# A two-layer streaming encoder step: after the attention, work that VectorE or GpSimd could do goes to VectorE alone; the norms add their squares with two additions

## The chip, the cores and the metric

The kernel runs on one core of one Trainium2 chip. The engines are named as the profile names them: PE is TensorE (matmuls; PEld is its weight load), DVE is VectorE, ACT is ScalarE, POOL is GpSimd, SP is SyncE, which issues the DMAs. The metric is device time in microseconds (us) of one execution, lower is better.

## The reference, cut to what matters

One inference step of two layers, for a prompt of 2048 frames and a sample of 32 frames with caches. D_MODEL is 1024, all data is f32.

```python
for l in range(DEPTH):                      # 2 layers
    hp = rms_norm(yp, ln_pre[l]); hs = rms_norm(ys, ln_pre[l])
    if l % 2 == 0:                          # layer 0: attention
        qa, ka, va, ga, qb, kb, vb, gb = ab_project(hp, pos_p, w_in_ab[j])
        oa = prompt_band(qa, ka, va, N_PREV_A, None, sinks_a[j])        # 8 heads, 2 KV heads, rotary, sinks
        ob = prompt_band(qb, kb, vb, N_PREV_B, relpos_b[j], None)       # 8 heads, learned bias
        mp = ab_output(oa, ob, ga, gb, w_out_ab[j])  # concat(oa*silu(ga), ob*silu(gb)) @ w_out
        ...                                 # the same for the sample, with caches
    else:                                   # layer 1: recurrence
        mp, h_last, conv_last = lru_mixer(hp, ...)
        ...
    yp = yp + rms_norm(mp, ln_post[l]); ys = ys + rms_norm(ms, ln_post[l])

def rms_norm(x, g):
    y = xf * lax.rsqrt(jnp.mean(xf * xf, axis=-1, keepdims=True) + EPS)
    return y * g

def lru_mixer(h, conv_state, h0, w_in, ...):
    xb, z = jnp.split(h @ w_in, 2, axis=-1)
    xc = conv_b + sum of 4 taps of xb * conv_w          # width-4 causal depthwise convolution
    r, gi = sigmoid(block-diagonal xc @ wa + ba), sigmoid(block-diagonal xc @ wx + bx)
    log_a = C_GATE * r * log_sigmoid(lam); a = exp(log_a)
    u = sqrt(-expm1(2 * log_a)) * (gi * xc)
    hs = scan of  h = a * h + u                         # along time
    return (hs * silu(z)) @ w_out, ...
```

## The kernel before, in words

Prompt and sample stand side by side as 2084 columns (tokens), with the 1024 channels on the partitions in 8 tiles of 128. The columns are cut into 6 blocks of 352 (the last 324), and two blocks make one part, b = 0, 1, 2. Each dense product is done with operands split in a high and a low piece: a weight tile of 128 output channels is `wh` and `wl` (`wh` is the weight rounded to the matmul's type, `wl` what is left), an input is `r0h`/`r0l` or `r1h`/`r1l`, and a result of one block is 8 channel tiles x 3 products (high x high, high x low, low x high) = 24 matmuls of 128x352 into an accumulator `acc` in PSUM.

The order of all instructions is made when the program is built, by a list scheduler (class `Sched`). Every piece of the work is a generator that yields requests (`R`) for an engine; the scheduler keeps an own clock per engine with a table of costs (`cost`), asks the waiting generators by priority, and gives a request to an engine when its inputs and buffers are ready. Where a request names two engines, `("V", "G")` for DVE or POOL or `("A", "V")` for ACT or DVE, `pick` takes the one that would end first by that table. Nothing is decided on the chip; each engine works through its own list in order, and waits on semaphores. All instructions go through one helper line, so the profile puts them all on L101, and groups are told apart by the names of the tiles.

The stages, by the program:

- Layer 0's input product for three parts, and the attention beside it and behind it (`soft`, `transp`: scores `S`, softmax rows `pt`, transposes `T`, outputs `O`). The key ("attention",) is set when the last attention piece has been scheduled. In the profile the last `pt` row is at 994 us.
- Layer 0's output product, parts 0 to 2 (`out_part`). `fin_out` takes each accumulator: ACT scales it into `m` and squares it (`tz`, `tzb`), the squares are added into `sacc`, and at the end of a block PE sums `sacc` over the partitions (`norm_sum`, by way of the split `xs`, into PSUM `misc`), ACT takes the root into `r`, DVE inverts it, and `m` is multiplied by `r` and the residual (`xr`, `eti`, `xt`) is added, in pieces of 5 and 3 channel tiles (880 and 528 columns). The weights of these stages still have to be split: `w_split` makes `wh` on ACT or DVE and `wl` on DVE or POOL, 1024 columns each, from the staged tile `wst`. There are three `wh`/`wl` pairs.
- `y_proc` makes the inputs of that product for parts 1 and 2 (products `xt<-xt`, `ex<-ex`, then the split into `r1h`/`r1l` or `r0h`/`r0l`).
- Layer 1, three times `in_part` and `out_part`. `in_part` is the input product with, for each of 8 channel tiles c: `fin_x` (ACT copies the accumulator to `xb`, DVE makes the convolution from `xb` in four instructions into a tile `xc`, which is shown as `ex`; split into `xs`; gate matmuls `g` with `gh`/`gl`; gates on ACT; the scan on DVE; the split into `r0h`/`r0l`), and `fin_z2` (the SiLU gate, which frees the accumulator on DVE). There is one `xb` buffer. The weights of part 0 are split here too, and stored for parts 1 and 2.
- `norm_proc` is the norm ahead of a layer, for one part: ACT squares half of a tile of [128, 8, 176] into `sq` (one buffer, 4 channel tiles x 176 columns), DVE sums it over the 4 channel tiles into `ss`, four times per block, then `norm_sum`, root, reciprocal and 8 scalings per piece. It runs for parts 1 and 2 in layer 0 and for parts 0 to 2 ahead of layer 1.

PE's list has no other source than this scheduler: when a weight or an accumulator is late, PE stands.

Of the kernel before, what the change touches and what calls it, by code (L numbers as in the profile page):

```python
# [12 lines left out]
OP = mybir.AluOpType  # L13
AX = mybir.AxisListType
# [45 lines left out]
def _cols(ap):  # L60
    n = 1
    for x in ap.shape[1:]:
        n *= x
    return n
# [19 lines left out]
class Eng:  # L84


    def __init__(self, sch, name, eng):
        self.sch, self.name, self.eng = sch, name, eng
# [77 lines left out]
class Sched:  # L166
# [3 lines left out]
    def __init__(self):  # L170
        self.t = {"PE": 0.0, "A": 0.0, "V": 0.0, "G": 0.0, "SP": 0.0, "DMA": 0.0}
        self.w, self.r, self.key = {}, {}, {}
        self.procs = []
        self.now = 0.0
        self.n = 0
        self.tab = None
        self.lock = {"V": [], "G": []}
        self.win, self.busy, self.half = 0, 0.0, False
        self.pem, self.vpt = PEMA, VPTA
        self.halves, self.cuts, self.loaded = set(), {}, set()  # L180
# [16 lines left out]
    def cost(self, e, op, outs, ins, a, k):  # L197
        n = max(_cols(x) for x in outs + ins) if e != "PE" else 0
        if e == "PE":
            m = ins[1]  # L200
            w = _cols(m)
            if op == "transpose":
                return ins[0].shape[0] / 1200.0 + 0.004
            return max(w / 2400.0 + 0.0133, 0.108) if m.dtype == F32R else 4 * w / 2400.0
        if e == "A":
            c = (0.104 if all(str(x.space).endswith("SB") for x in ins[:1]) else 0.067) + n / 1200.0 + 0.093 * sum(hasattr(k.get(x), "tensor") for x in ("scale", "bias", "accum_out"))
            f = a[2] if op == "activation" else None
            tab = "sqrt" if f == AF.Sqrt else "exp" if f in (AF.Exp, AF.Tanh) else None
            if tab and tab != self.tab:
                c += 1.3  # L210
                self.tab = tab
            return c
        if e == "V":
            if op == "reciprocal":
                return 0.06 + n * 0.0066
            if op in ("tensor_copy", "tensor_scalar", "memset") and all(str(x.space).endswith("SB") for x in outs + ins):
                return 0.06 + n * 0.00053 + self.vpt * sum(_cols(x) == 1 for x in ins[1:])
            if op == "tensor_tensor_scan":
                return 0.1 + n * 0.00115
            return 0.06 + n * 0.00106 + self.vpt * sum(_cols(x) == 1 for x in ins[1:])  # L220
        if op in ("tensor_scalar", "memset"):
            return 0.1 + n * 0.00106
        return 0.1 + n * 0.00223
# [57 lines left out]
    def set(self, key, t=None):  # L281
        self.key[key] = self.now if t is None else t
# [38 lines left out]
    def pick(self, req):  # L321

        t = self.avail(req)
        if t is None:
            return None
        if req.eng[0] == "SP" and req.ins and not isinstance(req.ins[0], tuple):
            t += SPM
        best = None
        for i, e in enumerate(req.eng):
            if e == "PE":  # L330
                if t <= self.now + EPSR / 2:
                    best = (0, e)
                continue
            if self.t[e] > self.now + LOOK[e] or t > max(self.now, self.t[e]) + EPSR:
                continue
            f = max(self.t[e], t) + (req.cost[i] if req.cost else 0.0) + (VPEN if e == "V" else 0.0)
            if best is None or f < best[0]:
                best = (f, e)
        if best and req.func and self.tab and req.func != self.tab:

            if req.since is None:
                req.since = self.now
            if self.now < req.since + 1.0:
                return None
        return best and best[1]
# [49 lines left out]
def hybrid_kernel(ctx, tc, I, O):  # L395
    nc = tc.nc
    sch = Sched()
    V, A, G, PE, SP = [Eng(sch, n, e) for n, e in (("V", nc.vector), ("A", nc.scalar), ("G", nc.gpsimd),
                                                  ("PE", nc.tensor), ("SP", nc.sync))]
# [215 lines left out]
    def cells_of(b):  # L615
        return [(bi, T0[2 * b + bi] + off, bi * BLK + off, w) for bi in range(2) for off, w in subs(2 * b + bi)]
# [43 lines left out]
    def norm_proc(src, b, gi, ri, key, rings, free=None, after=None, src_ready=(), then=None, blocks=(0, 1)):  # L660

        if after is not None:
            yield R("SP", [lambda: after])
        cells = cells_of(b)

        def block(bi, xs):
            cc = cells[2 * bi:2 * bi + 2]
            sa, sb = yield R("A", [xs[0]], [ssr, ssr])
            offs = [0, cc[0][3]]
            tot = cc[0][3] + cc[1][3]  # L670
            for x, (_, _, _, w), o in zip(xs, cc, offs):
                for ss, ks in ((sa, slice(0, 4)), (sb, slice(4, 8))):
                    sq, = yield R("A", [x], [sqr])
                    A.activation(sq[:, :, :w], x[:, ks, :w], AF.Square)
                    yield R("V", [sq])
                    V.tensor_reduce(ss[:, o:o + w], sq[:, :, :w].rearrange("p k t -> p t k"), AX.X, OP.add)
                    sqr.release(sq)
            e, _ = yield R(("G", "V"), [sa, sb], cost=(0.89, 0.43))
            ENG[e].tensor_tensor(sa[:, :tot], sa[:, :tot], sb[:, :tot], OP.add)
            ssr.release(sb)  # L680
            ps = yield from norm_sum(sa[:, :tot])
            r = sa
            yield R("A", [ps], func="sqrt")
            A.activation(r[:, :tot], ps[:, :tot], AF.Sqrt, bias=epsT, scale=1.0 / D)
            psr_.release(ps)
            for x, (_, _, _, w), o in zip(xs, cc, offs):
                yield R("V", [r])
                V.reciprocal(r[:, o:o + w], r[:, o:o + w])
                for k0 in (0, 4):
                    yield R("V", [r])  # L690
                    for k in range(k0, k0 + 4):
                        V.scalar_tensor_tensor(x[:, k, :w], x[:, k, :w], vec[:, gi, k:k + 1], r[:, o:o + w], OP.mult, OP.mult)
            ssr.release(sa)

        idx = [2 * bi + j for bi in blocks for j in range(2)]
        xs = {}

        def load(i, g):
            xs[i], = yield R("SP", src_ready, [g])
            x_load(xs[i], src, cells[i][1], cells[i][3])  # L700
        early = len(rings) == len(idx)
        for i, g in zip(idx, rings):
            yield from load(i, g)
        if early:
            for bi in blocks:
                yield from block(bi, [xs[2 * bi], xs[2 * bi + 1]])
        for bi in blocks:
            ii = (2 * bi, 2 * bi + 1)
            if not early:
                if bi == 1:  # L710
                    for i, g in zip(ii, rings):
                        yield from load(i, g)
                yield from block(bi, [xs[i] for i in ii])
            t = 0.0
            for i in ii:
                t = max(t, (yield from split_R(xs[i], cells[i][3], ri, cells[i][2], [(free, bi)] if free else [])))
                rings[idx.index(i) % len(rings)].release(xs[i])
            sch.set((key, bi), t)
        if then:
            then()  # L720
# [1229 lines left out]
    def dense_2():  # L1950
        for b in range(3):
            yield from out_part(b, base + 8 * b, b % 2, I["xT"], LN_POST, x2T, lambda k, bi, b=b: (("y", b), bi), late_m=b > 0)
            if b == 0:

                yield R("PE", [("attention",)])
        spawn(gw_proc(), 1)
        xrr.retire(eti)
        for x in extra:
            xtr.retire(x)
        b1 = base + 24  # L1960
        for b in range(3):
            yield from in_part(b, b1 + 24 * b, 1, 0)
            if b < 2:
                spawn(norm_proc(x2T, b + 1, LN_PRE + 1, 1, (1, b + 1), [xtr, xtr], free=("in", b), src_ready=[("x2", b + 1)]), PY3)
            yield from out_part(b, b1 + 24 * b + 16, 0, x2T, LN_POST + 1, O["yT"], lambda k, bi, b=b: ("yc", b, k), late=True, final=b == 2)
# [29 lines left out]
    ar, szr = [Ring(sch, None, None, None, t, 1, tiles=[x]) for t, x in zip(("a", "sz"), parts[1])]  # L1995
    xtr.idle += [(0.0, -1, x) for x in extra]
    sch.set(("attention",))
    sch.pem, sch.vpt = PEM, VPT
    spawn(y_proc(1, 1, ("y", 1), then=y2), PY2)
    sch.run(lambda: not sch.procs)  # L2000
# [114 lines left out]
```

## Time and profile before

| what | us |
|---|---|
| median of 3 runs | 1881.93 (1880.21 to 1882.59) |
| the profiled execution | 1876.91 |
| its span, first to last instruction | 1875.1 |
| what lies around the span | 1.8 |
| busy in the span: PE, DVE, ACT, POOL | 1743.0, 1590.4, 1002.5, 610.6 |

The profiled execution is 5.0 us below the median of the runs. PE is busy 93% of the span, but matmuls overlap, so this is no measure of how full PE is: where PE runs without a break a 352-column matmul starts every 0.16 us and each is shown with 0.32 us. PE's idle time and the granted clock (`PEclk`, a share of full speed) are what can be read.

A row of a table by stages gives for each stretch its length, the busy time of each engine (x instructions), the granted clock and the DMA share. A row of a table by tile gives engine, operation, what is written from what, how often, and the least, the median and the largest duration in ns. A row of waits gives who waited for whom, the sum in us, how often and the longest.

### The profile page before, as it was taken

Reading aid. Unit: us, or ns where it says so; the run is one execution under the profiler, and the core shown is the slowest. Engines: PE = TensorE matmul, PEld = TensorE weight load, DVE = VectorE, ACT = ScalarE, POOL = GpSimd, SP = SyncE. Lnnn points to the kernel's source line nnn. Section 1 sums busy time; section 2 is a strip of 40 time slices with the busy share of each in tenths; the row PEclk is TensorE's granted clock in tenths of the full one; section 3 lists DMA queues with packets and bytes.
Section 4 is the critical chain, followed back from the end, with each engine's and each line's share of the span. In section 5 each row is a group of like instructions: output and inputs, shape, how many; then the busy total and the mean of one; then the engine's idle time right before and its main releaser. Section 6 shows DMA issues by size and latency. Waiting matters only on the chain. (4 is left out here: it accounts for less than half of the span.)

```text
span 1875.1 us, 31799 instructions
## 1 busy us (share of the span) xinstructions
PE 1743.0 (93%) x11078; PEld 1686.8 (90%) x11078; DVE 1590.4 (85%) x3168; ACT 1002.5 (53%) x2048; POOL 610.6 (33%) x433
## 2 busy tenths in 40 slices
PE   8999999999999999999989969989889999999995
PEld 7999999889899999999979959988889999998995
DVE  8999967999999679989897879799898988699943
ACT  4276632476657337656564343456663586447831
POOL 4332214322223232221242646654423320153112
PEclk8999999999999999999999979999889999999997
DMA  5798856887554487877765884585455834565376
GB/s 177 205 252 262 233 151 211 228 249 211 168 157 119 128 237 186 245 202 203 212 190 153 225 231 134 191 258 175 154 174 186 238 121 149 182 200 167 128 269 177
DMA packets 293577, 362.80 MB, mean 193 GB/s; under 512 B 36309, under 2 KB 244617, under 8 KB 293401
## 3 DMA queue, kind: packets, MB, share of 16 engines
q1 hardware_dynamic: 293416, 360.78, 65.3%
q8 instruction: 87, 1.43, 0.3%
q14 instruction: 74, 0.60, 0.1%
HBM read 255.77 MB, written 107.00 MB: 193 GB/s over the span
## 5 line engine op out<-in xcount | busy, mean ns | idle before, releaser
L101 PE MATMUL acc<-r0h,wh 128*128 128x352 f32 (+2 forms) x1832 | 594.6, 325 | 16.3 <-ACT r0h L101 6.6
L101 PE MATMUL acc<-r0l,wh 128*128 128x352 f32 (+2 forms) x1832 | 595.1, 325 | 1.3 <-DVE r0l L101 1.3
L101 PE MATMUL acc<-r0h,wl 128*128 128x352 f32 (+2 forms) x1832 | 594.4, 324 | 1.5 <-DMA wl<-wo1s 1.5
L101 PEld LDWEIGHTS acc<-r0h,wh 128*128 128x128 f32 x1832 | 348.3, 190 | 19.4 <-ACT r0h L101 7.2
L101 PEld LDWEIGHTS acc<-r0l,wh 128*128 128x128 f32 x1832 | 348.2, 190 | 3.2 <-DVE r0l L101 2.2
L101 PEld LDWEIGHTS acc<-r0h,wl 128*128 128x128 f32 x1832 | 348.2, 190 | 3.2 <-DMA wl<-wo1s 2.5
L101 PE MATMUL acc<-r1h,wh 128*128 128x352 f32 (+1 forms) x864 | 282.8, 327 | 22.4 <-ACT xb L101 14.1
L101 PE MATMUL acc<-r1h,wl 128*128 128x352 f32 (+1 forms) x864 | 281.1, 325 | 15.2 <-POOL wl L101 15.2
L101 PE MATMUL acc<-r1l,wh 128*128 128x352 f32 (+1 forms) x864 | 281.0, 325 | 0.0
L101 POOL TENSOR_SCALAR pt<-pt,rr 128x256 f32<-128x256 f32 (+4 forms) x142 | 100.0, 715 | 366.2 <-DVE rr L101 214.3
L101 POOL TENSOR_TENSOR wl<-wst,wh 128x1024 fp32r<-128x1024 f32 x62 | 155.6, 2509 | 186.3 <-ACT wh L101 109.3
L101 ACT ACTIVATE pt<-pt,nm 128x256 f32<-128x256 f32 (+6 forms) x272 | 169.7, 626 | 61.2 <-DVE nm L101 59.3
L101 PEld LDWEIGHTS acc<-r1h,wh 128*128 128x128 f32 x864 | 166.1, 192 | 25.4 <-ACT xb L101 16.1
L101 PEld LDWEIGHTS acc<-r1h,wl 128*128 128x128 f32 x864 | 165.8, 192 | 15.5 <-POOL wl L101 15.5
L101 ACT CAST pp<-T 128x256 fp32r<-128x256 f32 (+4 forms) x314 | 134.0, 438 | 84.7 <-PE T L101 66.0
L101 PEld LDWEIGHTS acc<-r1l,wh 128*128 128x128 f32 x864 | 166.2, 192 | 0.0
L101 PE MATMUL T<-ident,pt 128*128 128x128 f32 (+2 forms) x864 | 143.4, 274 | 18.3 <-DVE pp L101 10.3
L101 DVE TENSOR_TENSOR pp<-T,pp 128x256 fp32r<-128x256 f32 (+4 forms) x314 | 150.4, 496 | 7.8 <-ACT pp L101 6.0
L101 PE MATMUL O<-pp,vt 128*128 128x256 f32 (+3 forms) x728 | 135.8, 309 | 10.0 <-DVE pp L101 4.7
L101 PEld LDWEIGHTS T<-ident,pt 128*128 128x128 f32 (+2 forms) x864 | 101.7, 140 | 42.7 <-DVE pp L101 19.9
L101 ACT CAST wh<-wst 128x1024 fp32r<-128x1024 f32 x70 | 73.5, 1049 | 99.7 <-PE acc L101 72.9
L101 PE MATMUL S<-kk,qa 128*128 128x320 f32 (+5 forms) x376 | 120.3, 334 | 3.6 <-issue 1.6
(252 smaller groups left out, 3312.8 us busy)
## 6 DMA issues: line engine op xcount, KB each, us to landing
wst<-w_in SPq DMA_DIRECT2D x93, 512.0 KB, 4.3
wst<-wo_in SPq DMA_DIRECT2D x32, 512.0 KB, 4.4
wh<-w1s SPq DMA_DIRECT2D x32, 512.0 KB, 3.7
wl<-w1s SPq DMA_DIRECT2D x32, 512.0 KB, 4.6
wh<-wo1s SPq DMA_DIRECT2D x24, 512.0 KB, 3.8
wl<-wo1s SPq DMA_DIRECT2D x24, 512.0 KB, 4.6
kk<-kB SPq DMA_DIRECT2D x32, 320.0 KB, 4.9
vt<-vB SPq DMA_DIRECT2D x16, 640.0 KB, 4.8
```

The costliest lines, as they stand in the source:

```text
L101: r = fn(*a, **k)
```

## The change

Three edits. First, the scheduler has a switch `alone`. While it is on, a request that names several engines is not given to POOL (requests that name POOL alone still are). It is set when the attention's end is reached, and in layer 1 it is turned off while an `in_part` has been issued and the following `out_part` is being issued: so it is on for layer 0's remaining output products, the norms between, and the three `in_part`s, and off for the three `out_part`s of layer 1. Second, in `norm_proc` the sum over 4 channel tiles, one strided `tensor_reduce` over 704 elements, becomes two additions: tiles 0 and 1 plus tiles 2 and 3 (352 columns, in place), then the two halves (176 columns). Third, the scheduler's table gets an own cost for the `tensor_reduce` that is left, in the first norm. The first edit as it acts in the order: 149 two-engine instructions leave POOL's list behind the attention, 23 stay.

```diff
@@ class Sched
+        self.alone = False
...
+            if op == "tensor_reduce":
+                return 0.06 + n * 0.00195
...
@@ pick
+            if e == "G" and len(req.eng) > 1 and self.alone:
                 continue
...
@@ norm_proc
                     yield R("V", [sq])
-                    V.tensor_reduce(ss[:, o:o + w], sq[:, :, :w].rearrange("p k t -> p t k"), AX.X, OP.add)
+                    V.tensor_tensor(sq[:, 0:2, :w], sq[:, 0:2, :w], sq[:, 2:4, :w], OP.add)
+                    V.tensor_tensor(ss[:, o:o + w], sq[:, 0, :w], sq[:, 1, :w], OP.add)
...
@@ dense_2
         for b in range(3):
+            sch.alone = True
             yield from in_part(b, b1 + 24 * b, 1, 0)
+            sch.alone = False
...
     sch.set(("attention",))
+    sch.alone = True
```

Since the scheduler's table decides the whole order, the rows move everywhere; buffer numbers differ from the start. Three places matter here.

**Layer 0's output product, part 1, the end of part 0's blocks.** POOL's list before (`m` is the product's output, `r` its inverse root, `eti` and `xr` the residual, `r0l` a low piece of part 2's input, `wl` the low piece of a weight):

```order
L101 TENSOR_TENSOR m_1_10371<-m_1_10371,r_0_10374 128x5x176
L101 TENSOR_TENSOR r0l_150<-ex1_0_10792,r0h_149 128x4x176
L101 TENSOR_TENSOR m_1_10371<-m_1_10371,r_0_10374 128x5x176
L101 TENSOR_TENSOR m_1_10371<-m_1_10371,eti_0_10782 128x5x176
L101 TENSOR_TENSOR r0l_150<-xt_0_151,r0h_149 128x4x176
L101 TENSOR_TENSOR sacc_0_10372<-sacc_0_10372,tzb_0_10779 128x352
L101 TENSOR_TENSOR m_1_10371<-m_1_10371,xr_0_153 128x5x176
L101 TENSOR_TENSOR r0l_150<-xt_1_152,r0h_149 128x4x176
L101 TENSOR_TENSOR wl_2_124<-wst_1_118,wh_2_121 128x1024
```

The same `wl` in DVE's list of the change:

```order
L101 RECIPROCAL r_0_10390<-r_0_10390 128x176
L101 TENSOR_TENSOR m_0_10386<-m_0_10386,xr_0_153 128x5x176
L101 TENSOR_TENSOR m_1_10387<-m_1_10387,r_0_10390 128x5x176
L101 TENSOR_TENSOR m_1_10387<-m_1_10387,r_0_10390 128x3x176
L101 RECIPROCAL r_0_10390<-r_0_10390 128x176
L101 TENSOR_TENSOR m_0_10386<-m_0_10386,xr_0_153 128x3x176
L101 TENSOR_TENSOR m_1_10387<-m_1_10387,r_0_10390 128x5x176
L101 TENSOR_TENSOR m_1_10387<-m_1_10387,r_0_10390 128x3x176
L101 TENSOR_TENSOR xt_0_151<-xt_0_151 128x704
L101 TENSOR_TENSOR wl_2_124<-wst_1_118,wh_2_121 128x1024
```

The `wl` was the last of a row of POOL's work that DVE shared; now it stands in one list with all of it, behind all eight products with `r` and four additions, ahead of the four other additions.

**The norm ahead of layer 1, part 0.** DVE's list before:

```order
L101 TENSOR_REDUCE ss_0_155<-sq_0_154 128x176
L101 TENSOR_REDUCE ss_1_156<-sq_0_154 128x176
L101 TENSOR_TENSOR sacc_0_10372<-sacc_0_10372,tzb_0_10779 128x352
L101 TENSOR_REDUCE ss_0_155<-sq_0_154 128x176
L101 TENSOR_REDUCE ss_1_156<-sq_0_154 128x176
```

and in the change:

```order
L101 TENSOR_TENSOR sq_0_154<-sq_0_154 128x352
L101 TENSOR_TENSOR ss_0_155<-sq_0_154 128x176
L101 TENSOR_TENSOR sq_0_154<-sq_0_154 128x352
L101 TENSOR_TENSOR ss_1_156<-sq_0_154 128x176
L101 TENSOR_TENSOR sacc_0_10388<-sacc_0_10388,tzb_0_10795 128x352
L101 TENSOR_TENSOR sq_0_154<-sq_0_154 128x352
L101 TENSOR_TENSOR ss_0_155<-sq_0_154 128x176
L101 TENSOR_TENSOR sq_0_154<-sq_0_154 128x352
L101 TENSOR_TENSOR ss_1_156<-sq_0_154 128x176
L101 TENSOR_TENSOR ss_0_155<-ss_0_155,ss_1_156 128x352
```

Each reduction is two rows, and the addition of the two halves `ss`, which stood on POOL, follows on DVE.

**Layer 1's first `in_part`.** POOL's list before held the weights' and the gates' low pieces and half of the splits `xs`:

```order
L101 TENSOR_TENSOR wl_0_122<-wst_1_118,wh_0_119 128x1024
L101 TENSOR_TENSOR xs_1_10789<-ex0_0_10791,xs_1_10789 64x704
L101 TENSOR_TENSOR wl_1_123<-wst_0_117,wh_1_120 128x1024
L101 TENSOR_TENSOR gl_0_10786<-gst_0_10790,gh_0_10785 128x256
L101 TENSOR_TENSOR wl_2_124<-wst_1_118,wh_2_121 128x1024
L101 TENSOR_TENSOR xs_0_10788<-ex0_0_10791,xs_0_10788 64x704
```

In the change they stand in DVE's list, between the convolution's instructions (`ex0<-xb,vec`):

```order
L101 TENSOR_TENSOR gl_0_10802<-gst_0_10806,gh_0_10801 128x256
L101 COPY hist_135<-xb_0_10803 128x3
L101 TENSOR_SCALAR ex0_0_10807<-xb_0_10803,vec_125 128x704
L101 TENSOR_TENSOR wl_0_122<-wst_1_118,wh_0_119 128x1024
L101 SCALAR_TENSOR_TENSOR ex0_0_10807<-xb_0_10803,vec_125,ex0_0_10807 128x704
L101 TENSOR_TENSOR wl_1_123<-wst_0_117,wh_1_120 128x1024
L101 SCALAR_TENSOR_TENSOR ex0_0_10807<-xb_0_10803,vec_125,ex0_0_10807 128x704 x2
L101 CAST xs_0_10804<-ex0_0_10807 64x704
L101 CAST xs_1_10805<-ex0_0_10807 64x704
L101 TENSOR_TENSOR xs_0_10804<-ex0_0_10807,xs_0_10804 64x704
```

Two `wl` have moved in among the four instructions that hold the one `xb`.

More of the change, by code (lines that the diff above doesn't have):

```diff
@@ L332, in pick @@
                     best = (0, e)
+                continue
+            if e == "G" and len(req.eng) > 1 and self.alone:
                 continue
```

## The prediction

> **What bounds the kernel now.** I read the page's first part, then the table by stages, then PE's waits in the stretch that the change reaches, then the tile tables and the timeline of the engines that PE waits for.
>
> ```profile
> span 1875.1 us, 31799 instructions
> PE 1743.0 (93%) x11078; PEld 1686.8 (90%) x11078; DVE 1590.4 (85%) x3168; ACT 1002.5 (53%) x2048; POOL 610.6 (33%) x433
> ```
>
> By the page PE bounds, DVE is close behind, and POOL is idle two thirds of the time, which would make it the engine to give work to. The stages tell more. Columns: stretch, length, busy PE, PEld, DVE, ACT, POOL, clock, DMA.
>
> ```profile
> 0.00:1000.00 1000.00, 956.18 (x6275) 912.88 (x6276) 876.11 (x2337) 550.06 (x1356) 286.70 (x261) 0.99 0.70 199
> 1000.00:1100.00 100.00, 84.52 (x524) 83.90 (x523) 79.33 (x64) 35.61 (x68) 57.85 (x28) 0.93 0.80 226
> 1100.00:1230.00 130.00, 119.86 (x733) 118.29 (x732) 109.70 (x113) 50.07 (x88) 76.83 (x41) 0.96 0.62 183
> 1230.00:1367.00 137.00, 119.95 (x701) 117.83 (x700) 125.70 (x130) 92.55 (x118) 63.35 (x30) 0.94 0.57 193
> 1367.00:1440.00 73.00, 63.51 (x362) 61.79 (x361) 60.66 (x82) 34.76 (x56) 13.41 (x9) 0.91 0.52 179
> 1440.00:1575.00 135.00, 128.17 (x785) 126.38 (x784) 121.31 (x150) 84.87 (x112) 39.16 (x23) 0.99 0.53 162
> 1640.00:1775.00 135.00, 129.54 (x824) 127.54 (x824) 126.96 (x185) 89.79 (x144) 46.48 (x27) 1.00 0.55 168
> 1775.00:1876.00 101.00, 77.10 (x491) 74.86 (x489) 44.32 (x52) 30.04 (x57) 20.32 (x10) 0.89 0.68 212
> 1000.00:1876.00 876.00, 786.78 (x4805) 773.94 (x4803) 714.28 (x832) 452.43 (x694) 323.92 (x172) 0.95 0.60 187
> ```
>
> The first row is the part up to the attention's end. 1000 to 1230 is the rest of layer 0's output product, 1230 to 1367, 1440 to 1575 and 1640 to 1775 are the three in_parts, 1367 to 1440 an out_part, and the last 101 us the last out_part. Behind the attention PE is idle for 876.0 - 786.8 = 89 us, and up to 1440 the clock is lowered as well. DVE and POOL together are busy 714.3 + 323.9 = 1038 us in 876. Whom PE waits for there, with the sum, the count and the longest:
>
> ```profile
> PE acc L101 <- POOL wl L101: 15.2, 1, 15.2
> PE acc L101 <- ACT xb L101: 14.1, 6, 4.9
> PE acc L101 <- DVE ex L101: 8.3, 3, 4.7
> PE acc L101 <- ACT r0h L101: 6.6, 2, 5.7
> PE g L101 <- DVE xs L101: 6.4, 7, 1.6
> PE misc L101 <- DVE xs L101: 6.1, 2, 5.8
> ...
> PE misc L101 <- POOL xs L101: 1.1, 1, 1.1
> ```
>
> These make 57.8 us; nearly all end with DVE or POOL, since xb is copied by ACT only when DVE has finished with the one buffer. So PE stands for the pair DVE and POOL. Now the pair, by tile, with the least, median and largest duration in ns:
>
> ```profile
> L101 POOL TENSOR_TENSOR wl<-wst,wh x24: 2372/2548/3253, 1020.9 to 1402.4; 128x1024 fp32r<-128x1024 f32 x24
> L101 DVE TENSOR_TENSOR wl<-wst,wh x20: 1209/1224/3149, 1006.2 to 1417.3; 128x1024 fp32r<-128x1024 f32 x20
> L101 DVE TENSOR_TENSOR m<-m,r x24: 1004/2332/2671, 1059.0 to 1861.8; 128x880 f32<-128x880 f32 x10, 128x528 f32<-128x528 f32 x10, 128x810 f32<-128x810 f32 x3, 128x486 f32<-128x486 f32 x1
> L101 POOL TENSOR_TENSOR m<-m,r x24: 1326/2217/2835, 1058.8 to 1863.6; 128x528 f32<-128x528 f32 x10, 128x880 f32<-128x880 f32 x10, 128x486 f32<-128x486 f32 x3, 128x810 f32<-128x810 f32 x1
> L101 DVE TENSOR_TENSOR m<-m,xr x15: 696/1078/2195, 1065.7 to 1697.4; 128x880 f32<-128x880 f32 x9, 128x528 f32<-128x528 f32 x4, 128x810 f32<-128x810 f32 x2
> L101 POOL TENSOR_TENSOR xs<-ex,xs x19: 1640/2233/2478, 1246.2 to 1771.9; 64x704 fp32r<-64x704 f32 x12, 64x676 fp32r<-64x676 f32 x7
> L101 DVE TENSOR_TENSOR xs<-ex,xs x29: 855/886/2020, 1235.1 to 1772.8; 64x704 fp32r<-64x704 f32 x20, 64x676 fp32r<-64x676 f32 x9
> L101 POOL TENSOR_TENSOR gl<-gst,gh x22: 737/1316/1874, 1220.9 to 1770.1; 128x256 fp32r<-128x256 f32 x22
> L101 DVE TENSOR_TENSOR gl<-gst,gh x2: 425/426/426, 1548.0 to 1749.0; 128x256 fp32r<-128x256 f32 x2
> L101 DVE SCALAR_TENSOR_TENSOR ex<-xb,vec,ex x72: 844/946/3075, 1230.9 to 1769.9; 128x704 f32<-128x704 f32 x48, 128x676 f32<-128x676 f32 x24
> L101 DVE TENSOR_TENSOR sacc<-sacc,tz x29: 459/518/2725, 1000.8 to 1842.3; 128x352 f32<-128x352 f32 x23, 128x324 f32<-128x324 f32 x6
> ```
>
> POOL takes about twice DVE's time for the same work, and DVE's own instructions have two durations: m with r is 1.0 us at the least and 2.3 in the median. The timeline shows which (start and length in us):
>
> ```profile
> 1062.42 2.79 POOL L101 TENSOR_TENSOR m<-m,r 128x880 f32<-128x880 f32 x1 [2.17 <-DVE r L101]
> 1063.19 2.58 DVE L101 TENSOR_TENSOR m<-m,r 128x528 f32<-128x528 f32 x1
> 1320.47 3.06 POOL L101 TENSOR_TENSOR wl<-wst,wh 128x1024 fp32r<-128x1024 f32 x1 [0.73 <-ACT wh L101]
> 1321.22 3.08 DVE L101 SCALAR_TENSOR_TENSOR ex<-xb,vec,ex 128x704 f32<-128x704 f32 x1
> ```
>
> A DVE instruction that meets one of POOL's lasts until POOL's is over and then its own time: 1062.42 + 2.79 = 1065.21, and 0.6 us more is DVE's end at 1065.77; likewise 1323.53 and 0.8 more. So with two SBUF inputs the two take turns, and what POOL does is paid by DVE at POOL's slower rate. DVE's 714 us hold much of such waiting.
>
> **The change part by part.** *DVE alone.* 149 instructions leave POOL (the part on the change counts them): 23 wl, 40 additions and products on m, 19 xs, 22 gl, 25 others of 648 to 704 columns, 16 sacc, 4 smaller. On DVE, undisturbed: 23 x 1.22 + 40 x 0.85 (half way between 1.0 for 880 columns and 0.7 for 528) + 44 x 0.886 + 22 x 0.426 + 20 x 0.52 = 28.1 + 34.0 + 39.0 + 9.4 + 10.4 = 121 us, in place of some 285 of POOL's 323.9 (23 stay, at 1.7 us or so, between the medians of gl and of m). That is 0.42 us for each us of POOL. It is free only if DVE's waiting falls by as much. I can't sum that waiting from one row. Bounds: at the most all 285, at the least none; from the m and r row alone (24 x about 1.5 us over the 0.7 to 1.0 undisturbed) come 28, and the rows of xb and wl show the same tail, so I take about 100, and expect DVE as busy as now.
>
> What PE gains, wait by wait:
>
> - The wl wait. PE stood from 1075 to 1090:
>
> ```profile
> 1087.71 2.81 POOL L101 TENSOR_TENSOR wl<-wst,wh 128x1024 fp32r<-128x1024 f32 x1
> 1090.57 0.66 PE L101 MATMUL acc<-r1h,wl 128*128 128x352 f32 x1 [15.21 <-POOL wl L101]
> 1057.43 1.25 DVE L101 RECIPROCAL r<-r 128x176 f32<-128x176 f32 x1 [2.28 <-ACT r L101]
> ```
>
>   In the new list this wl stands 18 instructions behind the first reciprocal: 4 reciprocals x 1.25, 6 m of 880 columns x 1.0, 6 of 528 x 0.7, 2 of 704 x 0.886, the wl 1.22, together 18.2 us. From 1057.4 that is 1075.6, when PE runs dry. The wait falls from 15.2 to between 0 and 4: 13. Late next is the following wl, three rows on (3.0 us); a weight feeds 48 matmuls (7.7 us), so it is in time.
> - xb and ex, 14.1 + 8.3 = 22.4. All have the convolution or the gate product stretched ahead of them (the 3.08 above instead of 0.95, ahead of a PE wait of 4.9). Bounds: 0, since two wl now stand among the four convolution instructions (2 x 1.22), and 19. Half: 11.
> - misc on xs, 6.1 + 1.1. The second edit and the addition of ss on DVE shorten the chain ahead of it: 3.
> - r0h, g on xs (6.6 + 6.4): chains with one or two POOL pieces in them; a third: 4.
> - The clock. (1 - clock) x length is 7.0 + 5.2 + 8.2 + 6.6 = 27 us up to 1440, part of it inside the waits. It is low around them. With about half the waits gone: 4.
>
> Sum 13 + 11 + 3 + 4 + 4 = 35.
>
> Against that, DVE's one list. Priced without any relief, moved POOL time x 0.42 on DVE's busy time against the stretch: 1230 to 1367, 125.7 + 26.6 = 152 for 137, +15; 1100 to 1230, 109.7 + 32.3 = 142 for 130, +12; 1640 to 1775, 127.0 + 19.5 = 146.5 for 135, +11.5; 1000 to 1100, +3.6; 1440 to 1575, 137.8 for 135, +2.8. That is 45 at the worst. The relief covers it on average; since work now queues in front of each other I charge a fifth: 9. Layer 1's out_parts keep POOL, and the last 101 us are as before.
>
> *The two additions.*
>
> ```profile
> L101 DVE TENSOR_REDUCE ss<-sq x40: 1268/1429/1469, 137.8 to 1633.9; 128x176 f32<-128x704 f32 x32, 128x162 f32<-128x648 f32 x8
> L101 DVE SCALAR_TENSOR_TENSOR xt<-xt,vec,ss x112: 373/391/2554, 162.5 to 1646.6; 128x176 f32<-128x176 f32 x96, 128x162 f32<-128x162 f32 x16
> ```
>
> The 352-column addition is priced by sacc, 0.52; the 176-column one by the nearest row, 0.39: 0.91 for 1.43, so 0.5 less, 40 times, 20 us of DVE, of which a wait shows only the misc item. 16 of the 40 lie ahead of 1000, where PE is busy 96%: worth 1, between 0 and 8.
>
> [...]
>
> *The cost of tensor_reduce* and all else that the new order reshuffles ahead of 1000: 0, within 5 either way; POOL's list there is 10 shorter. The sum is 35 + 1 - 9 = 27 against the profiled 1876.9, so 1850; the median of the runs stands 5.0 above that execution: 1855.
>
> **The rivals.**
>
> *DVE becomes the bound (slower).* If DVE's stretching is not POOL's doing, or what is saved goes to worse queueing, the 45 above are paid and the wl wait is still saved: 1881.9 + 45 - 13 = 1914; with half the relief 1892. It decides in the in_parts: above 135 us of DVE in 135 it wins. For it speaks that DVE is already at 127 there; against it the two-fold durations above. [...] Chance 0.14.
>
> *Hidden anyway.* The waits only move: PE runs dry elsewhere, xb is held longer by the wl among the convolution. Then the wl wait (13) and the charge (9) remain: 4 gained, 1878. For it: in_part's PE share is already 95% from 1440 on. Chance 0.16, of which 0.06 within 0.2%.
>
> *All of it.* The charge is nothing, the xb and ex waits go but 3, the clock is back: 15 + 19 + 5 + 8 + 8 = 55 gained, 1827. Chance 0.08.
>
> **How the numbers follow.** The forecast, 12 to 45 us gained, 1837 to 1870, has 0.62. 0.2% is 3.8 us, about what a measurement of this kernel tells from no change. Faster by more: 0.62 + 0.08 + 0.10 of the second rival = 0.80; within: 0.06; slower: 0.14. The range for 8 in 10: 1834, where the full gain begins to count, to 1881, which takes in the hidden case.
>
> **What would show it.** In the changed kernel's profile: POOL busy about 40 us behind the attention; m with r at 0.7 to 1.1 on DVE in layer 0; DVE busy 680 to 750 there; no PE wait on wl over 5 us; the convolution's largest under 2 us in the in_parts; reductions replaced by pairs of about 0.9. Wrong it would be if DVE is above 95% in an in_part with PE's waits on xb longer than 22 us in sum, or if the part ahead of 1000 moved by more than 8 us.

## The result, and the profile after

The changed kernel took 1833.27 us in the median of 4 runs (1827.26 to 1840.37), the kernel before 1882.26 us beside it: a ratio of 0.9743, 95% interval 0.9705 to 0.9781. On another chip, later, it was 0.9767 (0.9740 to 0.9794). The forecast was 1855.0, from 1834 to 1881: the direction was right, and the gain, 49 us, was nearly twice the 27 forecast and 0.7 us beyond the range. The profiled execution took 1835.62 us, 2.3 above that median; the one of before stood 5.4 below its own, so the two profiles differ by 41 us and not by 49. Two single executions further down, one of 4075 us and one of 2128, stand far off the others of their kernels and are not counted.

The page's first part:

```profile
span 1833.8 us, 31731 instructions
PE 1735.4 (95%) x11078; PEld 1678.0 (92%) x11078; DVE 1547.9 (84%) x3372; ACT 1001.9 (55%) x2045; POOL 316.6 (17%) x274
```

The table by stages with the columns of before (stretch, length, busy PE, PEld, DVE, ACT, POOL, clock, DMA), cut at the same events, and last everything behind the attention's end in one row:

```profile
0.00:1009.50 1009.50, 957.67 (x6275) 913.39 (x6276) 882.37 (x2358) 553.27 (x1361) 277.42 (x251) 0.99 0.70 197
1009.50:1106.00 96.50, 92.87 (x574) 91.97 (x573) 75.54 (x99) 40.22 (x74) 0.94 (x1) 0.98 0.88 251
1106.00:1217.00 111.00, 107.98 (x685) 107.40 (x684) 97.25 (x158) 48.21 (x85) 0.00 (x0) 1.00 0.64 192
1217.00:1330.00 113.00, 105.42 (x642) 101.90 (x641) 108.03 (x156) 88.82 (x112) 0.00 (x0) 1.00 0.63 217
1330.00:1400.00 70.00, 68.48 (x417) 67.95 (x416) 58.15 (x96) 34.86 (x57) 10.68 (x7) 0.98 0.67 228
1400.00:1536.00 136.00, 129.90 (x786) 126.45 (x785) 120.28 (x176) 84.45 (x110) 2.72 (x2) 0.99 0.52 160
1600.00:1733.00 133.00, 131.09 (x828) 129.08 (x827) 122.79 (x212) 88.71 (x145) 2.63 (x2) 1.00 0.56 171
1733.00:1834.00 101.00, 78.01 (x483) 75.89 (x481) 41.52 (x50) 29.03 (x54) 16.72 (x8) 0.90 0.66 212
...
1009.50:1834.00 824.50, 777.75 (x4805) 764.65 (x4803) 665.56 (x1015) 448.66 (x686) 39.14 (x23) 0.98 0.63 199
```

Two things stand here. Behind the attention the same 4805 matmuls take 824.5 us instead of 876.0, and DVE, which took over 149 instructions, is busy 665.6 us instead of 714.3: less, not more. The clock, 0.91 to 0.96 up to the first out_part before, is 0.98 to 1.00. And the first row, 6275 matmuls as before, now needs 1009.5 us instead of 1000: the part that the switch doesn't reach lost 9.5 us. PE's waits behind the attention (sum, count, longest):

```profile
PE g L101 <- DVE xs L101: 9.6, 13, 3.3
PE acc L101 <- DMA wl<-wo1s: 4.7, 3, 2.5
PE acc L101 <- ACT tz L101: 3.6, 3, 2.1
...
PE acc L101 <- DVE ex L101: 1.6, 1, 1.6
PE g L101 <- DVE gl L101: 1.6, 1, 1.6
PE acc L101 <- DVE wl L101: 1.6, 1, 1.6
PE acc L101 <- DVE r0h L101: 1.0, 1, 1.0
```

The wait for a wl that an engine makes (15.2) is 1.6, those for xb (14.1) are gone, those for ex (8.3) are 1.6, those of `misc` for xs (7.2) are gone. All of PE's waits here, with those that the prediction had no term for, went from 72.9 to 30.7 us. And the tiles (least, median and largest duration in ns):

```profile
L101 DVE TENSOR_TENSOR wl<-wst,wh x43: 1158/1219/2780, 1015.8 to 1380.0; 128x1024 fp32r<-128x1024 f32 x43
L101 DVE TENSOR_TENSOR m<-m,r x44: 657/996/2675, 1067.1 to 1820.5; 128x880 f32<-128x880 f32 x19, 128x528 f32<-128x528 f32 x19, 128x810 f32<-128x810 f32 x4, 128x486 f32<-128x486 f32 x2
L101 DVE TENSOR_TENSOR xs<-ex,xs x48: 855/885/890, 1217.2 to 1727.6; 64x704 fp32r<-64x704 f32 x32, 64x676 fp32r<-64x676 f32 x16
L101 DVE SCALAR_TENSOR_TENSOR ex<-xb,vec,ex x72: 912/943/953, 1212.2 to 1724.2; 128x704 f32<-128x704 f32 x48, 128x676 f32<-128x676 f32 x24
L101 DVE TENSOR_TENSOR sq<-sq x40: 466/517/2252, 141.2 to 1592.7; 128x352 f32<-128x352 f32 x32, 128x324 f32<-128x324 f32 x8
L101 DVE TENSOR_TENSOR ss<-sq x40: 327/342/827, 141.7 to 1593.2; 128x176 f32<-128x176 f32 x32, 128x162 f32<-128x162 f32 x8
```

The convolution's largest went from 3075 ns to 953, the product with r from a median of 2332 to 996. The second, longer duration is gone where POOL is silent: from 1017 to 1356 us POOL has no instruction, and the longest product with r takes 1065 ns there. The last two rows are the pair that replaced the reduction, over the whole kernel: 0.517 + 0.342 = 0.86 us for 1.43.

### The profile page after: what moved, and what is told of

It reads as the page before. It is cut to its first block, busy times and chain, and to the rows that moved or that the text cites. A ratio compares the mean times of both kernels' runs of the same rounds, so it can differ in the third digit from the quotient of the medians.

```text
span 1833.8 us, 31731 instructions
## 1 busy us (share of the span) xinstructions
PE 1735.4 (95%) x11078; PEld 1678.0 (92%) x11078; DVE 1547.9 (84%) x3372; ACT 1001.9 (55%) x2045; POOL 316.6 (17%) x274
## 3 DMA queue, kind: packets, MB, share of 16 engines
q8 instruction: 87, 1.43, 0.3%
## 4 chain that ended last, share of the span: by engine, by line
PE 42%; DVE 22%; DMA 7%; ACT 5%; issue 4%; POOL 1%; SPq 0%; DVEq 0%; ACTq 0%; POOLq 0%
PE acc L101 31%; PE O L101 4%; PE T L101 3%; PE S L101 3%; DVE ex L101 3%; DVE pt L101 3%; DVE m L101 2%; DVE ti L101 2%; DMA xr<-x2T 2%; DVE pp L101 2%; DVE eti L101 2%; DMA wl<-wo1s 1%; DVE ot L101 1%; DVE xs L101 1%; DMA x2T<-m 1%
## 5 line engine op out<-in xcount | busy, mean ns | idle before, releaser
L101 PE MATMUL acc<-r1h,wh 128*128 128x352 f32 (+1 forms) x864 | 278.5, 322 | 5.3 <-ACT tz L101 3.6
L101 POOL TENSOR_SCALAR pt<-pt,rr 128x256 f32<-128x256 f32 (+5 forms) x134 | 95.1, 721 | 420.8 <-DVE rr L101 256.1
L101 DVE CUSTOM_DVE_ANT_0 pt<-S,bias 128x320 f32<-128x320 f32 (+2 forms) x240 | 108.7, 479 | 21.2 <-PE S L101 15.1
L101 PEld LDWEIGHTS O<-pp,vt 128*128 128x128 f32 (+1 forms) x728 | 106.1, 193 | 19.8 <-DVE ot L101 5.9
```

The costliest lines, as they stand in the source:

```text
L101: r = fn(*a, **k)
```

## The experiments

Theory 1: POOL's instructions hold DVE up, and taking them away shortens DVE's own by more than the moved work costs. Theory 2: the additions did it. Theory 3: the new order of the lists did it, whoever works. Ratios are to the kernel before on the same chip. The table splits each profile at four events that all kernels share (the start of the last `pt` row, and of ACT's first `xb` in each of layer 1's parts), up to the last engine instruction; it is read off the traces, in us. Kernels whose lists agree up to the attention's end differ in the first column by up to 3.5 us, so less than that says nothing:

| kernel | to the attention's end | to part 0 | to part 1 | to part 2 | to the end |
|---|---|---|---|---|---|
| before | 994.6 | 215.5 | 236.4 | 206.8 | 214.9 |
| changed | 1004.1 | 192.8 | 210.0 | 205.9 | 213.9 |
| changed, again | 1003.9 | 191.6 | 208.3 | 204.5 | 208.6 |
| switch alone | 995.0 | 194.4 | 210.6 | 205.4 | 207.8 |
| additions and entry | 1003.3 | 211.3 | 225.3 | 204.1 | 214.6 |
| additions alone | 988.6 | 212.3 | 234.5 | 203.1 | 215.6 |
| entry alone | 988.7 | 209.4 | 234.6 | 206.8 | 213.5 |
| switch and additions | 992.1 | 191.9 | 210.2 | 205.2 | 208.4 |
| same, again | 991.8 | 191.1 | 210.2 | 205.0 | 208.6 |
| old lists, DVE issues | 992.1 | 206.4 | 224.3 | 204.0 | 210.0 |
| new lists, POOL issues | 1004.9 | 202.5 | 223.8 | 211.8 | 217.8 |
| switch to part 0's end | 994.7 | 195.7 | 210.7 | 208.0 | 215.8 |
| switch never off | 992.8 | 194.5 | 210.7 | 215.0 | 209.7 |

**The switch alone, and the norms' edits alone.** The first drops the additions and the table's entry; the second drops the two lines in `pick`.

> The first edit alone: the switch, with the norms' reductions and the table as before, so that everything up to the attention's end (994.6 us in the profile before) is the list of before. Theory 1 (POOL's two-input instructions hold DVE up; taken away, DVE's instructions are short and PE is fed in time): the loss of about 9 us ahead of the attention's end goes, nearly all of the 50 us behind it stays: 1826 (1820 to 1834). Theory 2 (the gain behind the attention is the additions' doing, by a shorter norm ahead of layer 1): at least 15 us of it go, 1845 or more.

Measured: 0.9731 (0.9710 to 0.9752), 1821.81 us for 1873.62, as theory 1 expected.

> The second and third edit alone: two additions and the cost of the remaining reduction, POOL as before. Theory 1: about 9 us later at the attention's end, a few us back behind it: 1886 (1880 to 1892). Theory 2: 1865 or less.

Measured: 0.9961 (0.9946 to 0.9976). Theory 2 falls: without the additions nothing is lost. The expectation of the second run was wrong as well, by some 11 us (a ratio of 1.002 was meant): the attention's end did come 9 us later, but behind it, by the table, 18 us came back in place of "a few".

**The old lists, issued to DVE.** The scheduler still believes that POOL works:

```diff
+    GV = Eng(sch, "G", nc.vector)      # booked as POOL, issued to DVE
+        def __getitem__(self, e):
+            return GV if e == "G" and sch.alone else dict.__getitem__(self, e)
```

> The scheduler and all lists of before, PE's and ACT's word for word; only, where the switch would be on, an instruction that the scheduler gave to POOL is issued to DVE at the same place. So the planner doesn't know of it. Theory 1: DVE's instructions become short, PE's waits on wl, xb and ex shrink without a new order: 1845 (1832 to 1860). Rival, theory 3 (the new order is what gains, DVE's list only carries it): DVE gets about 120 us more work that the planner didn't see, 1880 to 1900.

Measured: 0.9862 (0.9842 to 0.9883), 1849.19 us, inside theory 1's range. PE's waits on wl, xb and ex, 15.2, 14.1 and 8.3 before, are 8.8, 4.4 and 6.9.

**The new lists, given back to POOL.**

```diff
+            if f < max(self.t["V"], t) + c["V"]:    # f: end on a shadow clock of POOL
+                self.give, self.shadow = True, f    # booked as DVE, issued to POOL
```

> The changed kernel's scheduler and its lists for PE, ACT and SP word for word; only, while the switch is on, an instruction that could go to either is issued to POOL when POOL would end first by the table (a shadow clock), as the old rule would. POOL should again be busy over 200 us behind the attention. Theory 1: DVE is held up again, 1875 (1865 to 1895). Theory 3: the order keeps the gain, 1835 to 1845.

Measured: 0.9978 (0.9964 to 0.9991), 1869.72 us, as theory 1 expected, so nearly the whole gain is gone with the lists of PE, ACT and SP unchanged. The wait that grew is that of the gate matmuls for xs, 29.0 us in sum for 9.6. The stretch behind the attention in one row, first with the old lists on DVE:

```profile
992.00:1842.70 850.70, 786.21 (x4845) 776.19 (x4843) 679.61 (x983) 454.93 (x699) 44.09 (x28) 0.97 0.62 193
```

and with the new lists on POOL:

```profile
1005.00:1868.00 863.00, 794.90 (x4843) 782.21 (x4841) 692.68 (x891) 450.10 (x690) 279.04 (x153) 0.96 0.60 191
```

The product with r by tile, again first with the old lists on DVE:

```profile
L101 DVE TENSOR_TENSOR m<-m,r x44: 660/1000/2671, 1054.4 to 1830.6; 128x880 f32<-128x880 f32 x19, 128x528 f32<-128x528 f32 x19, 128x810 f32<-128x810 f32 x4, 128x486 f32<-128x486 f32 x2
```

and with the new lists on POOL:

```profile
L101 POOL TENSOR_TENSOR m<-m,r x24: 1316/2156/2814, 1069.0 to 1856.3; 128x528 f32<-128x528 f32 x19, 128x486 f32<-128x486 f32 x4, 128x880 f32<-128x880 f32 x1
L101 DVE TENSOR_TENSOR m<-m,r x24: 1003/1856/2974, 1069.6 to 1854.6; 128x880 f32<-128x880 f32 x19, 128x810 f32<-128x810 f32 x4, 128x528 f32<-128x528 f32 x1
```

With the old lists DVE does all the work in 679.6 us, less than the 714.3 it needed with POOL's help, and its products are at 1.0 us. That alone is worth 1.4%. The new lists without the relief (with the norms' edits in them) are worth 0.2%. Both together are worth 2.3 to 2.7%: the other half of the gain comes from a scheduler that knows who works, and it exists only on top of the relief. Theory 1 stands; theory 3 is right about that half and wrong as a rival. One thing these two runs don't separate: a moved instruction also takes half the time on DVE (`wl` 1.22 us for 2.55), so PE gets it sooner even where nothing is held up. That DVE's busy time falls is the relief alone, and the runs with a load below show what being held costs by itself.

**A load on POOL that nobody needs.** To size a turn, the switch alone with 60 idle instructions on POOL at the attention's end:

```diff
+    for _ in range(60):
+        nc.gpsimd.tensor_tensor(da, da, db, OP.mult)              # two inputs
+        nc.gpsimd.tensor_scalar(da, da, db[:, 0:1], 0.5, OP.mult, OP.mult)   # the other run: one input
```

> The first edit alone, its lists untouched, and beside them 60 additions of idle work on POOL at the attention's end: products of two SBUF tiles of 704 columns (about 1.67 us each, some 100 us from 995 on) on tiles that nothing else uses then, so nothing waits for them but DVE, if the two engines take turns. Theory 1: DVE's two-input instructions between 995 and 1095 become as long as in the kernel before (m with r about 2.3 instead of 1.0 us), 10 to 30 us are lost against the first edit alone: ratio to before 0.979 to 0.990. If turns are not what holds DVE: 0.973.

> The same with 60 instructions that read one tile (a scaling of 704 columns by a column and a constant) in place of the products. Theory 1 in the form of the prediction (two SBUF inputs take turns): DVE's durations and the time are those of the first edit alone, ratio 0.973. Theory 1b (any POOL instruction on SBUF holds DVE): as the run with products, in proportion to POOL's busy time.

Measured: 1.0235 (1.0212 to 1.0258) and 0.9982 (0.9966 to 0.9998). Part of both is an artefact of the tile chosen: `eti` also receives the residual by DMA, so SP's list, and with it a weight, stood behind POOL (DVE waited 52.0 us for its transfer in the first, and stood from 1048.5 to beyond 1080 us in the second), and PE had one wait of 57.8 us and of 42.6 us. Against the switch alone the two lost 94 and 47 us. They are repeated with another tile, `ti`:

> The run with 60 idle products on POOL once more, on a tile that no transfer is written to. In the earlier run one of the two tiles was also a landing place of the residual, so SP's list and a weight's transfer stood behind POOL for 52 us; that must be gone now. What is left is DVE's own stretching between about 1011 and 1130: two-input instructions last as long as POOL's product and then their own time (about 2.4 for 0.89, 2.5 for 1.22, 2.0 for 0.52). Theory 1: DVE has about 80 us of work there, stretched about twofold for 120 us of POOL; 25 to 60 us are lost against the first edit alone, ratio 0.986 to 1.005. If DVE's stretching were covered by other work: 0.973 to 0.976.

Measured: 1.0111 (1.0093 to 1.0129), more than expected. The timeline of DVE under this load (start and length in us):

```profile
1024.13 2.39 DVE L101 TENSOR_TENSOR ex<-ex 128x704 f32<-128x704 f32 x1
1026.45 2.16 DVE L101 CAST wh<-wst 128x1024 fp32r<-128x1024 f32 x1
1028.53 2.39 DVE L101 TENSOR_TENSOR r1l<-ex,r1h 128x704 fp32r<-128x704 f32 x1
```

The table of this kernel for 100 us under the load:

```profile
1010.00:1110.00 100.00, 62.03 (x314) 59.39 (x313) 96.58 (x46) 18.91 (x35) 96.39 (x47) 0.81 0.46 136
```

The same stretch with the switch alone and no load:

```profile
1010.00:1110.00 100.00, 94.39 (x586) 93.00 (x585) 81.48 (x104) 44.72 (x80) 0.00 (x0) 1.00 0.97 281
```

Each of DVE's seven two-input instructions from 1020 to 1036 us is held by about 1.5 us: 0.89 becomes 2.39, and a cast, which has one input and takes 0.69 otherwise, becomes 2.16. A reciprocal, one input as well, keeps its 1.24 us beside POOL: in the kernel before, the one at 1072.27 stands wholly inside a POOL instruction of 2.19 us that began at 1071.73. DVE gets 46 instructions done in 100 us instead of 104, and 0.038 of the ratio (71 us) goes for 127 us of POOL, in which POOL's own waiting for DVE is counted: 2.12 us a product in the mean, where in the run on `eti` 19 of them took 1.62 each from 1100 us on while DVE stood.

> The same with 60 scalings that read one tile. The earlier run showed DVE's additions at 1.46 instead of 0.88 in about half the cases, beside 69 us of POOL. So POOL's one-input instructions take turns as well, but once for each of DVE's pairs: 15 to 20 us of DVE time between 1011 and 1080. Theory 1 (any turn counts by its length): 3 to 15 us lost against the first edit alone, ratio 0.975 to 0.981. Theory 1 in the form of the prediction (only two inputs count): 0.973.

> The 60 scalings that read one tile, for their rows: the earlier run's ratio was 0.9845, 21 us above the first edit alone for about 69 us of POOL. Theory 1b (one-input instructions take turns too): DVE's additions of 704 columns at 0.88 and 1.46, stretched by 15 to 25 us in sum between 1011 and 1080, ratio 0.983 to 0.986. If the loss has another cause, DVE's rows there are as in the first edit alone.

Measured: 0.9845 (0.9828 to 0.9861) and 0.9826 (0.9801 to 0.9851), 18 to 21 us above the switch alone, more than the 3 to 15 expected of the first, so one input is enough. DVE's rows in the second:

```profile
1027.80 1.21 DVE L101 TENSOR_TENSOR wl<-wst,wh 128x1024 fp32r<-128x1024 f32 x1
1028.94 1.45 DVE L101 TENSOR_TENSOR r1l<-xt,r1h 128x704 fp32r<-128x704 f32 x1
1030.31 0.88 DVE L101 TENSOR_TENSOR xt<-xt 128x704 f32<-128x704 f32 x1
1031.12 1.09 DVE L101 TENSOR_TENSOR sacc<-sacc,tzb 128x352 f32<-128x352 f32 x1
```

Of DVE's 28 instructions from 1013 to 1045 us 16 are held, 13 of them by 0.4 to 0.6 us. The prediction's "with two SBUF inputs the two take turns" was too narrow: a two-input instruction of 704 columns takes 1.45 us for 0.88 beside one-input work, and the cast above, with one input, 2.16 for 0.69 beside two-input work.

**The additions alone, the entry alone, and the switch with the additions.** Three combinations without one or the other of the last two edits:

> The two additions alone, without the table's new entry and without the switch. If the table's entry re-ordered the first part, the attention ends at 995 as before, and behind it the gain of the second and third edit together stays: ratio 0.990. If the additions did it (DVE takes more turns with POOL while they run), the attention ends at 1003 and the time is that of both edits, ratio 0.996.

Measured: 0.9961 (0.9949 to 0.9974). The attention ends at 988.6 as in the first half of the expectation, the time is that of the second, so neither is right: the 15 us by which it ends sooner than with the entry are not in the time.

> The table's entry alone, with the reductions and POOL as before. If the entry by itself re-orders the part up to the attention's end to its loss, that part ends at 1003 to 1005 instead of 992 to 995, and the time is 3 to 10 us more than before: ratio 1.002 to 1.006. If entry and additions only lose together: 992 to 996, ratio 0.999 to 1.001.

Measured: 0.9958 (0.9942 to 0.9975), faster where slower or no change was expected.

> The changed kernel without the table's new entry, so the switch and the two additions. If the entry is what made the part up to the attention's end 9 us longer (that part ended at 988.6 with the additions alone, at 1003 to 1005 wherever the entry is in), the attention ends at 989 and the time is 8 to 15 us below the changed kernel's: ratio 0.966 to 0.970. If the time comes back behind the attention, as it did in the runs without the switch (equal ratios 0.9961): 0.972 to 0.976.

Measured: 0.9685 (0.9665 to 0.9705), as expected if the entry is to blame.

> The changed kernel, on one chip with the version without the table's entry. It should come out as before: ratio 0.974 (0.970 to 0.978).

> The switch and the two additions without the table's entry, on the same chip as the changed kernel. If the entry costs what the attention's ends show (988.6 to 992.1 without, 1003 to 1005 with it): 8 to 14 us below the changed kernel, ratio 0.967 to 0.970. If that difference was one of chips: equal.

Measured, on one chip: 0.9767 (0.9740 to 0.9794) and 0.9696 (0.9668 to 0.9723), 1830.41 and 1815.53 us. So the changed kernel without its third edit beats both kernels. By the first column of the table above the attention ends at 989 to 995 without the entry, at 989 with the entry alone, and at 1003 to 1005 with entry and additions together. Where that comes from shows in PE's count of matmuls by stretch: of the changed kernel, of that without the entry, and of the entry alone:

```profile
0.00:250.00 250.00, 227.65 (x1383) 214.51 (x1384) 224.74 (x556) 127.12 (x321) 70.78 (x67) 0.97 0.72 213
250.00:540.00 290.00, 280.57 (x1849) 270.94 (x1848) 248.07 (x627) 158.00 (x385) 86.07 (x82) 1.00 0.74 206
```

```profile
0.00:250.00 250.00, 234.74 (x1468) 224.07 (x1469) 228.22 (x586) 132.58 (x340) 76.80 (x75) 0.98 0.76 223
250.00:540.00 290.00, 278.05 (x1821) 268.34 (x1820) 247.16 (x624) 154.75 (x372) 89.15 (x80) 0.99 0.72 201
```

```profile
0.00:250.00 250.00, 230.63 (x1425) 219.64 (x1426) 229.06 (x560) 128.44 (x329) 80.33 (x75) 0.99 0.74 220
250.00:540.00 290.00, 286.85 (x1897) 278.38 (x1896) 252.21 (x640) 159.64 (x388) 87.51 (x82) 1.00 0.73 206
```

The loss is made in the first 250 us: 1383 matmuls instead of 1468. The only reductions left in the changed kernel run in its first 34 us; three of the five are long ones of 1408 elements, two have 704 (`ss<-pt`, and `s<-pt` with 0.948):

```profile
L101 DVE TENSOR_REDUCE ss<-xt x2: 2661/2745/2829, 16.3 to 19.1; 128x352 f32<-128x1408 f32 x2
L101 DVE TENSOR_REDUCE ss<-pt x1: 949/949/949, 32.6 to 32.6; 128x352 f32<-128x704 f32 x1
```

The entry prices the long ones at 2.81 us instead of 1.55 (they take about 2.75, so it is the truer number), but the two others at 1.43 instead of 0.81 (they take 0.95, so there the old number was nearer): 1.43 is right for a sum over 4 channel tiles, and these sum over 2. The list that the scheduler makes from there is worse for PE. The entry alone loses there too (1425) and gets it back from 250 to 540 (1897 for 1821), where its kernel still has reductions of the norms to price; with the additions there are none, and only the loss is left. That the reductions still to price are the reason is not shown, and neither which of the five prices does the harm nor which instruction of those early lists is late was tried.

**How far the switch should reach.** One kernel turns it off for parts 1 and 2, one never turns it off:

```diff
-            sch.alone = True
+            sch.alone = b == 0          # the first run
-            sch.alone = False           # the second run: line left out
```

> The first edit, with the switch on only to the end of layer 1's part 0, so that parts 1 and 2, where no weights are split, share work between DVE and POOL again as before. From the stages of the two profiles (22.6 and 26.3 us gained up to that point, 0.9 and 1.0 behind it) the time is that of the first edit alone within 3 us: ratio 0.973 to 0.9745. If the relief counts in each in_part alike, 10 us or more are lost: 0.978 or more.

Measured: 0.9798 (0.9774 to 0.9822): 12 us lost where at most 3 were expected; the other half of the expectation, 0.978 or more, names the right size. By the table 8 of the 12 are lost in the last stage (215.8 for 207.8). The 3 came from one profile's last stage, 213.9 us; that of the same kernel on another chip is 208.6. PE's larger waits from 1401 on in this kernel (wh from DRAM among them), of which the switch alone has a sum of 0.8 on wh and none on xb:

```profile
PE acc L101 <- DMA wh<-wo1s: 5.2, 1, 5.2
PE acc L101 <- ACT xb L101: 3.1, 1, 3.1
```

> The first edit alone, with the switch never turned off again: layer 1's three out_parts are without POOL too (some 20 instructions, 40 us of POOL). Theory 1: DVE's stretching in the out_parts goes as well, and the weights that wait for it come a little sooner: 0 to 4 us less than the first edit alone, ratio 0.971 to 0.973. Rival: at the end of a part DVE and POOL share the last products with r and the additions, and DVE alone ends them later: 3 to 8 us more, 0.975 to 0.977.

Measured: 0.9798 (0.9778 to 0.9818), 12 us lost: the rival had the direction, but 3 to 8 us, and at the end of a part. By the table 9.6 of the 12 are lost between the starts of parts 1 and 2. PE's wait, and what DVE was doing ahead of it:

```profile
1409.83 0.66 PE L101 MATMUL acc<-r1l,wh 128*128 128x352 f32 x1 [7.06 <-DVE r1l L101]
```

```profile
1404.41 1.68 DVE L101 TENSOR_TENSOR m<-m,r 128x880 f32<-128x880 f32 x2
1406.01 1.25 DVE L101 RECIPROCAL r<-r 128x176 f32<-128x176 f32 x1
...
1407.28 1.69 DVE L101 TENSOR_TENSOR m<-m,r 128x880 f32<-128x880 f32 x2
1408.90 0.88 DVE L101 TENSOR_TENSOR r1l<-xt,r1h 128x704 fp32r<-128x704 f32 x1
```

The low piece of part 1's input, which POOL makes in the out_part when it may, stood in DVE's one list behind the output's products, and the in_part began without it. With its slow restart (last section) this one wait makes 9.8 us.

## Why the prediction was right in direction and short in size

By its own terms, from the two profiles:

| term | forecast | measured |
|---|---|---|
| wl wait | 13 | 13.6 (15.2 to 1.6) |
| xb and ex | 11 | 20.8 (22.4 to 1.6) |
| misc on xs | 3 | 7.2 (7.2 to 0) |
| r0h, g on xs | 4 | 2.4 (13.0 to 10.6) |
| clock | 4 | 9.0 (the same 4805 matmuls busy 786.8, now 777.8) |
| DVE's one list | -9 | -1.8 (all other waits of PE, 15.1 to 16.9) |
| ahead of 1000, with the additions | 1 | -9.5 |

The measured column makes 41.7; the profiles differ by 41.3, for 27 forecast. The other 7.7 us of the miss are how the two profiled executions stand to their medians (5.4 and 2.3 us, above), which no term could foresee; without them the time would have come out inside the range.

- **The step that failed** is "I take about 100, and expect DVE as busy as now". DVE's busy time fell from 714.3 to 665.6 although 121 us were moved to it and only 24 x 0.57 = 14 saved by the additions: the relief was 714.3 + 121 - 14 - 665.6 = 156 us. It paid for all of the moved work and left DVE 35 us freer even before the additions; the old lists on DVE, without the additions, give the same 156 (714.3 + 121 - 679.6). From the 100 followed the charge of 9, of which 1.8 can be found. The xb and ex waits were halved for a reason of their own, the two wl among the convolution's four instructions; they take their 2.4 us, but none of the six is held up any more, and 20.8 of 22.4 went. The two runs that swap only the engine show the relief as a cause: 1.4% with the old lists, and the gain lost when the work goes back to POOL. A slip on the way: "24 x about 1.5 us" is 36 and not 28; the rows give 24 x 1.2 (49.2 us in sum, some 20.5 undisturbed), so the 28 is right. The step from 28 in one row to 100 in all was a guess, and too low.
- **The wl wait** was right, in place and size: the walk through DVE's new list gave 0 to 4, and no wait on wl is left in layer 0; behind it the largest on a wl that DVE makes is 1.6.
- **Ahead of 1000** the term was 0 within 5, and the text named 8 as what would show it wrong: it was 9.5, to the worse. It was put down to reshuffling; the runs show entry and additions together as its cause. Without the entry the ratio is 0.9685 to 0.9696.
- **The additions** took the duration forecast, 0.86 for 0.91, and gave some 0.4% (0.9961 alone; 0.9685 and 0.9696 against 0.9731 with the switch), 7 to 9 us where 4 were given to them. The entry alone, which shortens no instruction, gains the same 0.4%, so how much of this is the shorter sum and how much a new order is not shown. The price of the sum over 4 channel tiles was the 1.43 measured before.
- **The rivals.** "All of it", 55 gained, is what happened behind the attention (51.5), at a chance of 0.08; the first part then took 9.5 back. "DVE becomes the bound" was out by its own test: DVE is at 108.0 of 113 us (96%) in the busiest in_part, but PE has no wait on xb. It does come true in one place, the out_parts, when the switch is left on there. Every run that gave POOL work beside a busy DVE lost against the switch alone (18 to 71 us with the loads on `ti`), but for the out_parts.
- **The clock** was undersized (9.0 for 4). The last section shows for one wait a slow restart that goes when the wait goes; that such restarts are all of the 9.0 is not shown.

## What to carry to other kernels

Where DVE and POOL share work as they do here, price POOL's work in DVE's time, not by who ends first: here POOL's 285 us behind the attention saved DVE 121 us of work and cost it 156 of waiting (both worked out above). Give POOL what DVE would do too late (the low piece of the next part's input in the out_parts), and tell the planner, for half of the gain lay in lists made for it. Measure each edit of a planner's table apart: here an entry that is truer for three instructions and less true for two made a worse order, which only a run without it shows.

## What the runs showed of the hardware

A wait of PE can cost more than its length. Behind the wait of 7.06 us above, matmuls of 352 columns start every 0.29 us instead of 0.16; the table just before the wait and just behind it (the clock is the third number from the end):

```profile
1400.00:1402.80 2.80, 2.54 (x14) 2.25 (x14) 2.80 (x5) 0.55 (x1) 0.00 (x0) 1.00 0.00 0
1409.80:1413.80 4.00, 3.97 (x13) 3.97 (x14) 1.69 (x2) 0.33 (x1) 0.00 (x0) 0.50 0.27 85
```

The first 19 matmuls take 5.7 us instead of 19 x 0.16 = 3.0, so 2.7 us come on top of the 7.06. And one-input work on POOL isn't free for DVE either: 98 us of it, by the trace, cost 18 to 21 us of the kernel's time, against 71 for 127 us of two-input work. A strided `tensor_reduce` of 704 elements takes 1.43 us when it sums over 4 and 0.90 to 0.95 us when it sums over 2.
